# A hybrid encoder layer: four result buffers for SSD, state clears behind their loop, weighted keys on two engines

## Chip, cores and metric

The kernel runs on one core of a Trainium2 chip. The metric is the device time of one execution in microseconds (us). The core's engines each work through a queue of their own, in order: TensorE (PE), VectorE (DVE), ScalarE (ACT), GpSimd (POOL) and SyncE (SP), which here only issues transfers; ScalarE issues some too.

## What is computed

One encoder layer on a sequence of 1024 tokens, 1024 channels, all float32. A normed and modulated input `h` is projected once, four token mixers read parts of the projection, and their outputs, 256 channels each, are normed and joined by one output projection; a SwiGLU feed-forward follows.

```python
h = rms_norm(x) * (1 + sc1) + sh1
u = h @ w_in
y_ssd = ssd_mixer(u[..., :OFF_NA], ...)
y_na = rms_norm(neighborhood_attention(u[..., OFF_NA:OFF_ML], na_rpb), na_norm_g)
y_ml = mlstm_mixer(u[..., OFF_ML:OFF_HY], ...)
y_hy = hyena_mixer(u[..., OFF_HY:], ...)
x = x + g1 * (concatenate([y_ssd, y_na, y_ml, y_hy], -1) @ w_out)
h = rms_norm(x) * (1 + sc2) + sh2
x = x + g2 * ((silu(h @ ffn_w_gate) * (h @ ffn_w_up)) @ ffn_w_down)
return rms_norm(x, final_norm_g)
```

The two mixers that the change touches are SSD and mLSTM. Both work in chunks of 128 tokens, forwards and backwards. In mLSTM a chunk's state is the sum over its tokens of weighted keys times values; the states run through a decay from chunk to chunk; a chunk's result is its queries times the state before it, plus the queries and keys of the chunk itself, weighted by exponentials, times the values. The result is divided by a norm, squared and normed per head, and gated.

## The kernel before

**Stages.** They are written in this order (L349 to L395): modulation and the first norm, Hyena, the projection for SSD (`project_ssd`), the second modulation with its sums, mLSTM's gates and rows, SSD, the projection for mLSTM (`project_ml`), mLSTM (`mlstm`, L1262), the projection for attention (`project_na`), attention and the output projection (`out_round`, L1569, for the mixers' results in the rounds n = 2, 0 and 1), and the feed-forward. The order in which an engine does its work is not the written one: a planner that estimates when each operand is ready interleaves the stages and writes a fixed order for each engine. On the chip an engine never skips an instruction that waits.

**Matrix products.** Float32 operands are split in a high and a low half (`hhi`, `hlo`; `whi`, `wlo`; `yh`, `yl`; `wowh`, `wowl`), and a product is three: high by high, low by high, high by low. L495 (`gemm_t`) and L507 (`gemm_n`) are the projections, with sums in `gps`; L1566 (`out_part`) is the output projection, with sums in `gps` as well. The halves are made by `split` (L233 on ScalarE casts the high one, L239 on VectorE subtracts for the low one).

**SSD's end.** `finish_mixer` (L863) is called by Hyena and by SSD: a root of the mean square (`fss`, `fmv`, `fmt`, `fmr`, L871 and the helper `rsqrt`, L248 to L254), a product on VectorE (L874), then for each of four quarters four transposes on TensorE (`yps`, L879), a copy on ScalarE into the staging tile `yst` (L880), and a store to `yt` in DRAM (L881). SSD's four quarters share one staging buffer (tag `sE`).

**mLSTM.** Three buffers `mkv` take keys and values (L1279); POOL clears the first state of either direction (`mpv`, L1275 and L1276), whose memory was SSD's. For each of 8 chunks POOL weighs the keys in two halves, one for each direction (`mkw`, L1283), and TensorE makes the chunk's states (`mcs`, L1288). After the decay (L1297, VectorE) comes the loop over chunks: `mS` (queries by keys, L1317), `mD` (the exponents, L1322 to L1324), `msd` (the exponential on ScalarE, L1326, and the product on VectorE, L1328), `mpi` (L1335) and `mpa` (L1341) on TensorE, their sum `mtt` on VectorE (L1336, L1342), the norm `mnd` (L1345 to L1347), and on POOL the division (`mhh`, L1349) and the sum of both directions (`my`, L1352). Behind the loop: squares (`msq`, L1356, ScalarE), their sums (`mss`, L1357, VectorE), `rsqrt` on all of it with a table load and a root on ScalarE (`mrv`, `mrt`, `mrr`, L248 to L254, L1359), the product with the gate `mog` (L1366, loaded at L1363) and with the root (L1368), transposes (`yps`, L1374), copies (L1375, three staging buffers) and stores (L1376).

**The output projection's round** loads two slices of weights (`wor`, L1553, scaled at L1554 by `g`), two of a mixer's result (`yr`, L1579) and in the first round the eight tiles of x (L1584); the sums are added to x on VectorE (L1589). The tiles `wor`, `yr`, `yh`, `yl`, `wowh`, `wowl` and x lie in memory that `hhi`, `hlo` and the projection's weights hold until project_na's last matmul. Three buffers in turn take `wor` and `yr`.

Of the kernel before, what the change touches and what calls it, by code (L numbers as in the profile page):

```python
# [9 lines left out]
F32 = mybir.dt.float32  # L10
F32R = mybir.dt.float32r
AF = mybir.ActivationFunctionType
ALU = mybir.AluOpType
# [4 lines left out]
P = 128  # L18
# [267 lines left out]
def build(nc, tc, d, out, dbg=None, dump=None):  # L286
    K = Net(nc, tc, d, out)
    with ExitStack() as es:
# [58 lines left out]
        with ExitStack() as e2:  # L347
# [15 lines left out]
            with ExitStack() as e3:  # L363
                hyena(K, Tags(rpool("hy", e3), n4=2, n2=8, yk=9, tab=3, tai=3, ks=2, rt=2), w0)
# [9 lines left out]
            with ExitStack() as e3:  # L374
                ssd(K, Tags(rpool("ss", e3), cb=6))
            project_ml(K)
            mlstm(K, Tags(rpool("ml", right), va=2))
            project_na(K)
        xr = pool("xr")
# [91 lines left out]
def w_group(K, n, gate=False, first=True):  # L471

    nc = K.nc
    whi, wlo = (K.wp.tile([P, NK, 288 if gate else 256], F32R, t, name=f"{t}{n}") for t in ("whi", "wlo"))
    for j in range(3 if gate else 2):
        w = P if j < 2 else N_GATE
        raw = K.wp.tile([P, NK, w], F32, "raw", name=f"raw{n}")
        nc.sync.dma_start(raw, K.d["w_in"][n + j] if j < 2 else K.d["w_gate"])
        c = slice(j * P, j * P + w)
        with K.first() if first else nullcontext():  # L480
            K.split(whi[:, :, c], wlo[:, :, c], raw, "act", "dve")
    return whi, wlo


def gemm_t(K, whi, wlo, j):

    nc = K.nc
    c = slice(j * P, (j + 1) * P)
    pss = []
    for h in range(2):  # L490
        t = slice(h * 512, (h + 1) * 512)
        ps = K.pg.tile([P, 512], F32, tag="g", name="gps")
        seq = [(w, x, k) for k in range(NK) for w, x in ((whi, K.hhi), (whi, K.hlo), (wlo, K.hhi))]
        for n, (w, x, k) in enumerate(seq):
            nc.tensor.matmul(ps, lhsT=w[:, k, c], rhs=x[k][:, t], start=n == 0, stop=n == len(seq) - 1)  # L495
        pss.append(ps)
    return pss
# [13 lines left out]
def conv3(K, pss, acc, pcol):  # L511

    nc, pc = K.nc, K.pc
    w0, w1, w2, b = (pc[:, pcol + i:pcol + i + 1] for i in range(4))
    m, a = ALU.mult, ALU.add
    with K.first():
        for h in range(2):
            nc.scalar.activation(acc[:, h * 512:(h + 1) * 512], pss[h], AF.Identity, bias=b, scale=w1)
        for o, s, w in ((acc[:, 1:513], pss[0], w0), (acc[:, 513:1024], pss[1][:, :511], w0),
                        (acc[:, 0:511], pss[0][:, 1:512], w2), (acc[:, 511:1023], pss[1], w2)):  # L520
            nc.vector.scalar_tensor_tensor(o, in0=s, scalar=w, in1=o, op0=m, op1=a)
# [299 lines left out]
def hyena(K, sp, w0):  # L821
    nc = K.nc
    V = nc.vector
    z = sp.tile([P, 8, 256], F32, "z")
    late = Late()
    for n in (1, 2, 0):
        whi, wlo = w0 if n == 1 else w_group(K, G_HY + 2 * n)
        for j in range(2):
            pss = gemm_t(K, whi, wlo, j)
            acc = K.so.tile([P, L], F32, "st", name="acc")  # L830
            conv3(K, pss, acc, PC_HYW + 4 * (2 * n + j))
            late.run()
            if n == 0:
                late.add(to_natural, K, acc, z, j)
            else:
                late.add(_natural, K, acc, K.gates[n - 1][j], 0)
    late.run()
    zj = [z[:, :, j * P:(j + 1) * P] for j in range(2)]
    for o in range(2):
        hyena_conv(K, sp, z, o)  # L840
        for j in range(2):
            gate = sp.tile([P, 8, P], F32, "gate")
            nc.sync.dma_start(gate, K.gates[o][j])
            V.tensor_tensor(zj[j], zj[j], gate, op=ALU.mult)
    finish_mixer(K, sp, zj, 2, "n2")


class Late:
# [11 lines left out]
        self.fn = None  # L860


def finish_mixer(K, sp, y, m, tag):  # L863

    nc = K.nc
    ss = sp.tile([P, 2, 8], F32, "fss")
    for i in range(8):
        for j in range(2):
            jk = sp.tile([P, P], F32, "jk", bufs=2)
            nc.scalar.activation(jk, y[j][:, i], AF.Square, accum_out=ss[:, j, i:i + 1])  # L870
    nc.vector.tensor_tensor(ss[:, 0], ss[:, 0], ss[:, 1], op=ALU.add)  # L871
    r = K.rsqrt(sp, ss[:, 0], [P, 8], 256, "fm")
    for j in range(2):
        nc.vector.tensor_tensor(y[j], y[j], r[:, :, None].broadcast_to([P, 8, P]), op=ALU.mult)  # L874
        for h in range(2):
            st = sp.tile([P, 512], F32, tag, name="yst")
            ps = K.pm.tile([P, 512], F32, "m", name="yps")
            for i in range(4):
                nc.tensor.transpose(ps[:, i * P:(i + 1) * P], y[j][:, h * 4 + i], K.ident)  # L879
            nc.scalar.copy(st, ps)  # L880
            nc.scalar.dma_start(K.yt[2 * m + j][:, h * 512:(h + 1) * 512], st)  # L881
# [142 lines left out]
def ssd(K, sp):  # L1024
    nc, d = K.nc, K.d
    V, G = nc.vector, nc.gpsimd
# [54 lines left out]
    pv = sp.tile([P, 8, 2, 2, 2, 64], F32, "spv")  # L1081
# [18 lines left out]
    for i in range(7):  # L1100
        for dr in range(2):
            c, n = (i, i + 1) if dr == 0 else (7 - i, 6 - i)
# [7 lines left out]
    y = pv.rearrange("p c g d h e -> p c (g d h e)")[:, :, 0:256]  # L1110
    for c in range(8):
# [17 lines left out]
        E = sp.tile([P, 512], F32, "sE")  # L1129
# [16 lines left out]
        op = K.pm.tile([P, 512], F32, "m", name="ops")  # L1146
# [12 lines left out]
        for dr in range(2):  # L1159
            G.tensor_tensor(yv, yv, t1v[:, :, dr], op=ALU.add)  # L1160
        V.tensor_tensor(yc, yc, zn, op=ALU.mult)
    finish_mixer(K, sp, [y[:, :, j * P:(j + 1) * P] for j in range(2)], 0, "sE")


def mlstm_rows(K, sp0, sp):
# [96 lines left out]
def mlstm(K, sp):  # L1262
    nc, d = K.nc, K.d
    V, G = nc.vector, nc.gpsimd
    en, wip, emp, dec, gr, M, noneh = K.en, K.wip, K.emp, K.dec, K.gr, K.M, K.noneh
# [6 lines left out]


    pv = sp.tile([P, 2, 8, 2, 65], F32, "mpv")
    G.memset(pv[:, 0, 0], 0.0)  # L1275
    G.memset(pv[:, 1, 7], 0.0)  # L1276
    for c in range(8):
        kv = kvs[c % 3]
        nc.sync.dma_start(kv[:, :, :, 0:64], K.mvk[:, c].rearrange("p n (h e) -> p n h e", h=4))  # L1279
        va, kn = kv[:, 0], kv[:, 1, :, 0:64]  # L1280
        kw = sp.tile([P, 2, 4, 64], F32, "mkw", bufs=2)
        for dr in range(2):
            G.tensor_tensor(kw[:, dr], kn, en[:, c, 2, dr][:, :, None].broadcast_to([P, 4, 64]), op=ALU.mult)  # L1283
        ps = K.pm.tile([P, 512], F32, "m", name="mcs")[:, :260].rearrange("p (d j e) -> p d j e", d=2, j=2)
        for dr in range(2):
            for h in range(4):
                q, j = h % 2, h // 2
                nc.tensor.matmul(ps[64 * q:64 * q + 64, dr, j], lhsT=kw[:, dr, h], rhs=va[:, h], start=True, stop=True)  # L1288
        if c < 7:
            nc.scalar.copy(pv[:, 0, c + 1], ps[:, 0])  # L1290
        if c > 0:
            nc.scalar.copy(pv[:, 1, c - 1], ps[:, 1])
    for i in range(7):
        for dr in range(2):
            c, n = (i, i + 1) if dr == 0 else (7 - i, 6 - i)
            for j in range(2):
                V.scalar_tensor_tensor(pv[:, dr, n, j], in0=pv[:, dr, c, j], scalar=dec[:, dr, c, j:j + 1],  # L1297
                                       in1=pv[:, dr, n, j], op0=ALU.mult, op1=ALU.add)
    y = sp.tile([P, 8, 256], F32, "my")
    for c in range(8):  # L1300
# [30 lines left out]
        for q in range(2):  # L1331
# [6 lines left out]
            for dr in range(2):  # L1338
                for j in range(2):
                    h = 2 * j + q  # L1340
# [28 lines left out]
    for j in range(2):  # L1369
        for h in range(2):  # L1370
            st = sp.tile([P, 512], F32, "msd", bufs=3, name="yst")
# [516 lines left out]
```

## Time and profile before

| | before |
|---|---|
| median of 3 runs | 1519.16 us (1516.4 to 1523.06) |
| the profiled execution | 1516.75 us |
| its span, first to last instruction | 1515.0 us |
| mean granted TensorE clock | 0.973 of full speed |
| TensorE busy | 1388.1 us (92%) |
| VectorE busy | 1114.9 us (74%) |
| ScalarE busy | 542.4 us (36%) |
| GpSimd busy | 90.5 us (6%) |

The span is 1.75 us shorter than the profiled execution's own time. Busy shares are averages over stages with different limits: what a change in one stage is worth is read from that stage's waits and from what stands next on the waiting engine. The stages in question lie between about 590 us (SSD's end) and 710 us (the first rounds of the output projection); mLSTM's first state matmul runs at 608.89 us and its last `mpa` at 674.53 us.

### The profile page before, as it was taken

The page shows a single profiled execution, that of the slowest core. Times are in us where ns is not written, and L with a number is a line of the kernel's source. Part 1 is how long each engine was busy: PE and PEld are TensorE (multiplying, and loading weights), DVE is VectorE, ACT ScalarE, POOL GpSimd, SP SyncE. Part 2 cuts the span into 40 slices and gives each one's busy share as a digit, 9 for nine tenths or more (in the row PEclk, how much of TensorE's full clock was granted, in tenths as well). Part 3 has the DMA queues.
Part 4 walks back from the last instruction along what each step waited for, and adds up shares of the span by engine and source line. Part 5 has one row for each costly group of instructions (what it writes and reads, how often), then busy time and mean ns, then how long its engine had stood idle before and what let it go on. Part 6 is the DMA issues. An engine that isn't in the chain of part 4 may idle for free.

```text
span 1515.0 us, 19511 instructions
## 1 busy us (share of the span) xinstructions
PE 1388.1 (92%) x6717; PEld 1114.2 (74%) x6717; DVE 1114.9 (74%) x2123; ACT 542.4 (36%) x973; POOL 90.5 (6%) x143
## 2 busy tenths in 40 slices
PE   2589989998988999989998999999999999999995
PEld 0366778777777768867776777887778778888884
DVE  7998977887846684587865468478778887557588
ACT  2522222232142343333546766322222222434352
POOL 2110000000100331330000000000000000000000
PEclk9889999999998999999999999999999999999998
DMA  6634367577673332566525458677776676977762
GB/s 249 197 97 150 119 198 222 184 237 232 204 243 100 104 101 91 157 221 209 163 91 189 143 175 278 237 253 247 261 247 223 229 266 240 327 239 243 245 210 111
DMA packets 160598, 300.31 MB, mean 198 GB/s; under 512 B 27871, under 2 KB 72831, under 8 KB 160500
## 3 DMA queue, kind: packets, MB, share of 16 engines
q1 hardware_dynamic: 137204, 271.77, 54.9%
q10 hardware_dynamic: 22688, 25.99, 4.9%
q0 software_dynamic: 608, 1.31, 0.3%
q8 instruction: 53, 0.87, 0.2%
q14 instruction: 45, 0.37, 0.1%
HBM read 221.12 MB, written 77.89 MB: 197 GB/s over the span
## 4 chain that ended last, share of the span: by engine, by line
PE 59%; DVE 14%; DMA 10%; issue 3%; ACT 2%; POOL 2%; SPq 0%; DVEq 0%; POOLq 0%; ACTq 0%
PE Z L1616 8%; PE X L1616 7%; PE dx L1854 6%; PE Y L1616 5%; PE gps L495 4%; PE gps L507 4%; PE dz L1854 4%; PE dy L1854 4%; PE gps L1566 3%; DMA wu<-wu 2%; DMA mxw<-modw 2%; PE nS L1429 2%; PE ops L1566 1%; PE nS L1407 1%; DMA mxacc<-macc 1%
## 5 line engine op out<-in xcount | busy, mean ns | idle before, releaser
L495 PE MATMUL gps<-hhi,whi 128*128 128x512 f32 x320 | 129.8, 406 | 3.8 <-ACT nt L531 3.8
L495 PE MATMUL gps<-hlo,whi 128*128 128x512 f32 x320 | 129.9, 406 | 0.0
L495 PE MATMUL gps<-hhi,wlo 128*128 128x512 f32 x320 | 129.3, 404 | 0.0
L239 DVE TENSOR_TENSOR dl<-dr,dh 128x1024 fp32r<-128x1024 f32 x77 | 93.8, 1221 | 40.7 <-ACT dh L233 32.4
L233 ACT CAST dh<-dr 128x1024 fp32r<-128x1024 f32 x77 | 80.6, 1052 | 108.9 <-PE dx L1854 28.4
L1616 PE MATMUL Z<-hp,wgh 128*128 128x512 f32 x352 | 95.5, 402 | 1.0 <-ACT ps L1671 0.7
L1616 PEld LDWEIGHTS Z<-hp,wgh 128*128 128x128 f32 x352 | 63.7, 188 | 19.0 <-ACT ps L1671 4.4
L507 PE MATMUL gps<-whi,hhi 128*128 128x256 f32 (+1 forms) x256 | 76.1, 297 | 1.5 <-ACT z L531 1.5
L507 PE MATMUL gps<-wlo,hhi 128*128 128x256 f32 (+1 forms) x256 | 77.0, 301 | 0.0
L507 PE MATMUL gps<-whi,hlo 128*128 128x256 f32 (+1 forms) x256 | 76.8, 300 | 0.0
L495 PEld LDWEIGHTS gps<-hhi,whi 128*128 128x128 f32 x320 | 60.6, 189 | 18.6 <-ACT nt L531 5.0
L495 PEld LDWEIGHTS gps<-hhi,wlo 128*128 128x128 f32 x320 | 60.5, 189 | 13.9 <-issue 2.0
L495 PEld LDWEIGHTS gps<-hlo,whi 128*128 128x128 f32 x320 | 60.6, 189 | 13.0 <-issue 1.3
L233 ACT CAST T3h<-wu 128x1024 fp32r<-128x1024 f32 x22 | 23.2, 1052 | 130.8 <-PE Y L1616 120.0
L1616 PE MATMUL X<-A,t4s 128*128 128x512 f32 x264 | 63.5, 389 | 1.3 <-DVE uv L1755 1.3
L1500 DVE SCALAR_TENSOR_TENSOR mxacc<-mxw,cond,mxacc 128x512 f32<-128x512 f32 x56 | 42.0, 750 | 28.2 <-DMA mxw<-modw 28.0
L1616 PEld LDWEIGHTS X<-A,t4s 128*128 128x128 f32 x264 | 49.5, 188 | 11.9 <-DVE uv L1755 1.7
L507 PEld LDWEIGHTS gps<-whi,hhi 128*128 128x128 f32 x256 | 50.4, 197 | 2.7 <-ACT z L531 1.9
L1854 PE MATMUL dx<-dh 128*128 128x512 f32 x132 | 51.3, 389 | 0.0
L1854 PE MATMUL dx<-dh,dl 128*128 128x512 f32 x132 | 51.3, 389 | 0.0
L1854 PE MATMUL dx<-dl,dh 128*128 128x512 f32 x132 | 51.3, 389 | 0.0
L507 PEld LDWEIGHTS gps<-wlo,hhi 128*128 128x128 f32 x256 | 50.2, 196 | 1.6 <-issue 0.7
(521 smaller groups left out, 3499.2 us busy)
## 6 DMA issues: line engine op xcount, KB each, us to landing
wg<-wg SPq DMA_DIRECT2D x44, 512.0 KB
mxw<-modw SPq DMA_DIRECT2D x64, 256.0 KB
raw<-w_in SPq DMA_DIRECT2D x28, 512.0 KB
dr<-wd SPq DMA_DIRECT2D x55, 256.0 KB
psd<-ps SPq DMA_DIRECT2D x22, 512.0 KB
psr<-psd SPq DMA_DIRECT2D x22, 512.0 KB
wu<-wu SPq DMA_DIRECT2D x22, 512.0 KB
ad<-a SPq DMA_DIRECT2D x22, 512.0 KB
```

The costliest lines, as they stand in the source:

```text
L233: nc.scalar.copy(hi, src)
L239: e.tensor_tensor(lo, src, hi.bitcast(F32), op=ALU.subtract)
L495: nc.tensor.matmul(ps, lhsT=w[:, k, c], rhs=x[k][:, t], start=n == 0, stop=n == len(seq) - 1)
L507: nc.tensor.matmul(ps, lhsT=x[k][:, t], rhs=w[:, k, :N], start=n == 0, stop=n == len(seq) - 1)
L1407: nc.tensor.matmul(pb[:, :nk], lhsT=qt[r, i], rhs=ktv[r, r0:r0 + nr, f * 24:f * 24 + 40], start=True, stop=True)
L1429: nc.tensor.matmul(pb[:, 448:512], lhsT=pT[:w * 40, n], rhs=vw[:w * 40, n, c:c + 64], start=n == 0, stop=n == len(chunks) - 1)
L1500: V.scalar_tensor_tensor(acc, in0=mt, scalar=K.cond[:, k:k + 1], in1=acc, op0=ALU.mult, op1=ALU.add)
L1566: K.nc.tensor.matmul(ps, lhsT=l, rhs=r, start=n == 0, stop=n == 5)
L1616: nc.tensor.matmul(ps, lhsT=w[a][:, k], rhs=x[k][b], start=start and n == 0, stop=n == 11, skip_group_check=not start)
L1854: nc.tensor.matmul(acc[i], lhsT=a[:, 0, ts], rhs=b[:, 1], start=first and m == 0, stop=final and m == 2, skip_group_check=n in (2, 3, 5, 6))
```

## The change

SSD's four quarters get four staging buffers, of the tags `sE`, `sW`, `sdm` and `sxd`, whose tiles SSD no longer needs by then; Hyena keeps its one. The two clears of `mpv` are written behind the loop over the states. The weighted keys of the second direction are made on VectorE. From L877 on lines of the changed kernel have a number one higher.

```diff
-    finish_mixer(K, sp, zj, 2, "n2")
+    finish_mixer(K, sp, zj, 2, (("n2", None),))
...
-def finish_mixer(K, sp, y, m, tag):
+def finish_mixer(K, sp, y, m, tags):
...
         for h in range(2):
-            st = sp.tile([P, 512], F32, tag, name="yst")
+            tag, bufs = tags[(2 * j + h) % len(tags)]
+            st = sp.tile([P, 512], F32, tag, name="yst", bufs=bufs)
...
-    finish_mixer(K, sp, [y[:, :, j * P:(j + 1) * P] for j in range(2)], 0, "sE")
+    finish_mixer(K, sp, [y[:, :, j * P:(j + 1) * P] for j in range(2)], 0, (("sE", None), ("sW", None), ("sdm", 2), ("sxd", 2)))
...
     pv = sp.tile([P, 2, 8, 2, 65], F32, "mpv")
-    G.memset(pv[:, 0, 0], 0.0)
-    G.memset(pv[:, 1, 7], 0.0)
     for c in range(8):
...
-        for dr in range(2):
-            G.tensor_tensor(kw[:, dr], kn, en[:, c, 2, dr][:, :, None].broadcast_to([P, 4, 64]), op=ALU.mult)
+        for dr, E in enumerate((G, V)):
+            E.tensor_tensor(kw[:, dr], kn, en[:, c, 2, dr][:, :, None].broadcast_to([P, 4, 64]), op=ALU.mult)
...
         if c > 0:
             nc.scalar.copy(pv[:, 1, c - 1], ps[:, 1])
+    G.memset(pv[:, 0, 0], 0.0)
+    G.memset(pv[:, 1, 7], 0.0)
```

The planner's orders differ from line to line much more than the text does. Three places follow. On TensorE, behind mLSTM's last chunk, there stood before:

```order
L1335 MATMUL mpi<-mpv,mqk 128x130 x2
L1341 MATMUL mpa<-mkv_5072,msd 128x65 x2
L1566 MATMUL gps<-wowh,yh 128x512
L1341 MATMUL mpa<-mkv_5072,msd 128x65 x2
L1335 MATMUL mpi<-mpv,mqk 128x130 x2
L1341 MATMUL mpa<-mkv_5072,msd 128x65 x4
L1566 MATMUL gps<-wowh,yl 128x512
L1566 MATMUL gps<-wowl,yh 128x512
```

and now, from the same point:

```order
L1336 MATMUL mpi<-mpv,mqk 128x130 x2
L1342 MATMUL mpa<-mkv_5072,msd 128x65 x4
L1336 MATMUL mpi<-mpv,mqk 128x130 x2
L1342 MATMUL mpa<-mkv_5072,msd 128x65 x4
L1375 MATMUL yps<-ident,my 128x128 x16
L1567 MATMUL gps<-wowh,yh 128x512 x3
L1567 MATMUL gps<-wowh,yl 128x512
L1567 MATMUL gps<-wowl,yh 128x512
```

Before, 40 matmuls of the output projection stood between the last `mpa` and the first transpose of `my`; now the 16 transposes follow the last `mpa` directly. Ahead of mLSTM, 108 `gps` of L507 stood between the last `gps` of L495 and the first `mcs`; now 60 do, and the other 48 stand among mLSTM's chunks.

On ScalarE, from the last `msd` of mLSTM to the casts of the output projection, before:

```order
L1326 ACTIVATE msd<-mD 128x512 x2
L1356 ACTIVATE msq<-my 128x256
L233 CAST yh<-yr 128x1024
L233 CAST wowh<-wor 128x1024
L1356 ACTIVATE msq<-my 128x256
L249 ACT_TABLE_LOAD
L249 ACTIVATE mrt<-mrv 128x32
L233 CAST wowh<-wor 128x1024
L1375 COPY yst<-yps 128x512
```

and now:

```order
L1327 ACTIVATE msd<-mD 128x512 x2
L1357 ACTIVATE msq<-my 128x256
L976 DMA vn<-no 40x4x256 x2
L1357 ACTIVATE msq<-my 128x256
L249 ACT_TABLE_LOAD
L249 ACTIVATE mrt<-mrv 128x32
L1376 COPY yst<-yps 128x512
L1377 DMA yt<-yst 128x512
L1376 COPY yst<-yps 128x512 x2
L1377 DMA yt<-yst 128x512 x2
L1376 COPY yst<-yps 128x512
L233 CAST wowh<-wor 128x1024
```

The first casts of the output projection (`wowh`, `yh`) moved from ahead of the table load, among mLSTM's last chunks, to behind the four copies of mLSTM's result.

On SP, the loads of mLSTM's last chunks and of the first round of the output projection, before:

```order
L1448 DMA g_6391<-gd 128x1024
L1553 DMA wor<-w_out 128x1024
L1303 DMA mqk<-mqk 128x512
L1306 DMA mkv_5072<-mvk 128x4x64
L1553 DMA wor<-w_out 128x1024
L1579 DMA yr<-yt 128x1024
L1584 DMA x_5_6278<-x 128x1024
L1303 DMA mqk<-mqk 128x512
L1584 DMA x_6_6279<-x 128x1024
L1363 DMA mog<-mon 128x512
```

and now:

```order
L1304 DMA mqk<-mqk 128x512
L1364 DMA mog<-mon 128x512
L1585 DMA x_0_6273<-x 128x1024
L1585 DMA x_1_6274<-x 128x1024
...
L1585 DMA x_6_6279<-x 128x1024
L1449 DMA g_6391<-gd 128x1024
L1554 DMA wor<-w_out 128x1024 x2
L1580 DMA yr<-yt 128x1024
L1585 DMA x_7_6280<-x 128x1024
L1580 DMA yr<-yt 128x1024
```

All loads of x, `g`, `wor` and `yr` now stand behind mLSTM's last load; before, five tiles of x, both `wor` and one `yr` stood ahead of it. The clears of `mpv` stand ahead of the first `mkw` in POOL's order, before and now.

## Rows read from the trace of the kernel before

**Rows 1.** The chain that ended last, whole execution, share by engine.

```profile
PE 59%; DVE 14%; DMA 10%; issue 3%; ACT 2%; POOL 2%; SPq 0%; DVEq 0%; POOLq 0%; ACTq 0%
```

**Rows 2.** Busy time per stretch: stretch, its length, PE, PEld, DVE, ACT, POOL, clock, DMA share, GB/s.

```profile
645.00:650.00 5.00, 4.73 (x31) 3.53 (x30) 4.91 (x14) 2.11 (x4) 1.99 (x3) 1.00 0.95 303
680.00:686.00 6.00, 5.41 (x13) 4.02 (x13) 3.67 (x7) 1.93 (x3) 2.64 (x3) 0.50 0.73 245
710.00:790.00 80.00, 79.95 (x415) 61.23 (x414) 60.74 (x165) 36.44 (x88) 0.00 (x0) 1.00 0.44 134
```

**Rows 3.** PE's waits, 585 to 720 us: line, waited for, total, times, longest.

```profile
PE gps L1566 <- DVE yl L239: 4.1, 3, 2.9
PE mcs L1288 <- POOL mkw L1283: 1.0, 1, 1.0
PE mpa L1341 <- ACT msd L1326: 0.8, 3, 0.3
PE yps L879 <- DVE spv L874: 0.6, 1, 0.6
```

**Rows 4.** The chain in order of time, from 600 us: start, length, what.

```profile
599.96 9.00 PE gps L507 x75
...
695.74 4.50 DMA yr<-yt
...
739.83 6.14 PE gps L1566 x27
```

**Rows 5.** PE's instructions, two chunks of mLSTM: start, length, engine, line, count.

```profile
631.29 0.71 PE L1317 MATMUL mS<-mqk 64*128 64x128 f32 x4
...
638.75 0.72 PE L1317 MATMUL mS<-mqk 64*128 64x128 f32 x8
...
644.75 0.72 PE L1317 MATMUL mS<-mqk 64*128 64x128 f32 x8
```

**Rows 6.** PE's instructions, end of mLSTM and first round; in brackets idle before.

```profile
674.53 1.11 PE L1341 MATMUL mpa<-mkv,msd 128*128 128x65 f32 x8
678.50 0.50 PE L1566 MATMUL gps<-wowh,yl 128*128 128x512 f32 x1 [2.86 <-DVE yl L239]
...
708.43 0.50 PE L1566 MATMUL gps<-wowh,yl 128*128 128x512 f32 x1 [0.64 <-DVE yl L239]
```

**Rows 7.** ACT's instructions.

```profile
594.89 0.59 ACT L880 COPY yst<-yps 128x512 f32<-128x512 f32 x1 [2.12 <-DMA yt<-yst]
...
684.48 0.23 ACT L249 ACTIVATE mrt<-mrv 128x32 f32<-128x32 f32 x1
...
705.29 1.99 ACT L233 CAST yh<-yr 128x1024 fp32r<-128x1024 f32 x2
```

**Rows 8.** POOL's instructions.

```profile
604.88 0.21 POOL L1275 MEMSET mpv<- 128x130 f32 x1 [18.40 <-DMA yt<-yst]
...
609.72 1.21 POOL L1283 TENSOR_TENSOR mkw<-mkv,men 128x256 f32<-128x256 f32 x2 [1.30 <-issue]
...
632.55 1.04 POOL L1349 TENSOR_TENSOR mhh<-mtt,mnd 128x512 f32<-128x512 f32 x1 [9.55 <-DVE mnd L1347]
633.67 0.88 POOL L1352 TENSOR_TENSOR my<-mhh 128x128 f32<-128x128 f32 x2
...
679.85 1.91 POOL L1349 TENSOR_TENSOR mhh<-mtt,mnd 128x512 f32<-128x512 f32 x1 [4.19 <-DVE mnd L1347]
681.84 0.87 POOL L1352 TENSOR_TENSOR my<-mhh 128x128 f32<-128x128 f32 x2
```

**Rows 9.** DVE's instructions.

```profile
589.11 0.20 DVE L250 RECIPROCAL fmr<-fmt 128x8 f32<-128x8 f32 x1 [1.15 <-ACT fmt L249]
...
631.40 0.43 DVE L1342 TENSOR_TENSOR mtt<-mtt,mpa 128x260 f32<-128x260 f32 x1
...
679.69 1.17 DVE L239 TENSOR_TENSOR yl<-yr,yh 128x1024 fp32r<-128x1024 f32 x1
...
690.61 2.78 DVE L1368 TENSOR_TENSOR my<-my,mrr 128x256 f32<-128x256 f32 x8
```

## Prediction

> **What bounds the kernel now.** I began with the chain that ended last: TensorE carries most of it [rows 1], so the question for every part of the change is whether PE's idle time grows or shrinks. Then one stretch without idle time behind the changed stages: from 710 to 790 us PE is busy 79.95 of 80 us at full clock [rows 2]. A microsecond that PE is late at 710 is therefore still missing at the end; no slack takes it up. Third, PE's waits between 585 and 720 us [rows 3]: only 0.6 us stand in SSD's finish (L879), where the first part of the change works; 1.0 stands at the state matmuls `mcs`, where the third part works, and 0.8 at `mpa`. The large one, 4.1 us in three pieces, stands behind mLSTM: the out-projection's first round waits for `yl`. The whole stock that the change aims at is thus below 3 us; what it could lose lies at the end of mLSTM. Fourth, the instructions themselves around 609 us [rows 4], in two chunks of mLSTM [rows 5], and at its end [rows 6].
>
> **SSD's four result buffers.** Before, ScalarE's second copy waits 2.12 us for the first store [rows 7], and the copies end late; POOL's `mpv` clears sit idle until 604.88 us for these stores [rows 8]. With four buffers those waits go. By themselves they are worth nothing: ScalarE has slack, and PE streams `gps` (project_na) all the while. What they do is let the planner start mLSTM sooner: on PE 60 `gps` of L507 stand behind the last one of L495 and ahead of the first `mcs`, where 108 stood. 48 fewer at 9.00 / 75 = 0.12 us [rows 4] is 5.76 us. Those 48 are not saved; they move into mLSTM's stage as filler, 72 in 25 pieces between the last `mcs` and the last `mpa`, where there were 24 in 5 pieces and four out-projection matmuls in 3.
>
> **The clears.** Written behind the loop, they still stand ahead of the weighted keys in POOL's order, so this part is costed at nothing; what covers it is that the clears take 0.21 us and the stores they wait for land sooner. If that cover goes, see the third rival.
>
> **The weighted keys.** A pair takes 1.21 us on POOL [rows 8]; with one half on DVE it takes the longer half, about 0.6 us, so `mcs` gets its keys 0.6 sooner. The DVE half of the same shape should be near the 0.4 us of DVE's other operations of this stage (`mtt`, [rows 9]); eight of them are 3.4 us of an engine that has gaps there. PE's 1.0 us wait can shrink by 0.6; ends 0 and 1.0. Beside this the trace shows the two engines in each other's way: POOL's `mhh` takes 1.91 us at 679.85, while DVE runs `yl` and `mnd`, against 1.04 at 632.55 [rows 8]. The Trainium skill (SBUF — State Buffer, "SBUF: two separate sides") speaks against the split: a DVE operation with two SBUF inputs and a GpSimd operation that reads SBUF exclude each other for a whole instruction. The trace agrees: `yl` ran from 679.69 for 1.17 us [rows 9], and 1.0 of it after `mhh`'s start is about what `mhh` took longer. By that rule the halves run one after the other, 0.4 + 0.6 us, the gain falls from 0.6 to 0.2 us, and the sum rises by 0.4.
>
> **Inside mLSTM.** The filler closes waits: 0.6 at `mcs` and 0.8 at `mpa`, together -1.4 (ends 0 and -1.8). Every piece of filler between the small matmuls also costs a break: the chunk from 631.29 to 638.75 us holds 8 `gps` in 4 pieces and takes 7.46 us, the next takes 6.00 [rows 5], of which 0.3 is a wait at `mpa` [rows 3]. 7.46 - 8 x 0.12 - 5.7 = 0.8, or 0.2 a piece; had the filler closed no wait, 0.12. I take 0.16. Twenty-five pieces against eight are +2.7 (ends 0 and 3.4). Net **+1.3**. So mLSTM's last `mpa` ends about when it did, 675.6 us [rows 6]: I call this T.
>
> **The end of mLSTM.** This is the term that decides. Before, the out-projection's loads and casts ran during mLSTM's last chunks, since project_na's last matmuls stood in mLSTM's second chunk and so freed the memory early; behind T, PE had 40 `gps` to do while DVE, POOL and ScalarE finished mLSTM's norm, and idled 4.1 us less the 0.64 at 708 us, 3.45 [rows 3, 6]. Now project_na's last matmul stands in the last but one chunk, all x, `wor` and `yr` loads stand on SP behind mLSTM's last load, and PE's order behind the last `mpa` is: all 16 transposes of mLSTM's result, then the first out-projection matmul. PE must sit through the whole chain, counted from T. From the start of `mtt` to the end of the second `my` it was 631.40 [rows 9] to 634.55 [rows 8] before: **3.2**. Square, sum, table load and root went from the end of `my` at 682.71 [rows 8] to 684.71 [rows 7]: **5.2**. Six small DVE operations at 0.2 each (as the reciprocal at 589.11 [rows 9]) make it **6.5**, eight products, 2.78 [rows 9], **9.3**. PE's transposes run half behind the first four products and half after the last, to **10.8**. ScalarE copies four results out; the fourth waits for a buffer (three exist) until the first store has landed, some 2.1 us after its copy (by the wait of 2.12 in [rows 7]), and ends at **11.7**. Only then come its casts `wowh`, `wowh`, `yh` at 1.0 each (`yh` x2, 1.99 [rows 7]), to **14.8**, where PE does three matmuls. DVE's `wowl`, `wowl`, `yl`, 1.2 each (`yl`, 1.17 [rows 9]), start when the first cast is done at 12.7 and end at **16.4**; PE gets three more. The second `yr` takes a buffer that the first `wowl` frees at 14, and a `yr` load took 4.50 [rows 4]: **18.5**; its cast and `yl` make **20.8**, and from there PE runs on.
>
> In those 20.8 us PE does 11 matmuls at 6.14 / 27 [rows 4] and 16 transposes, taken at the 0.12 of the 256-column `gps`, 4.4 us in all; idle is 16.4. Against 3.45 before: **+12.9**. Ends: +9 (the second `yr` and `yl` hidden) and +17 (loads late, below).
>
> **Clock.** After the gaps of before the granted clock is 0.50 from 680 to 686 us [rows 2], the 1.2 GHz level, with PE idle for 2.86 us ahead of it: some 3 us lost. The gap is longer now and the same slow stretch follows: **+0.3** (ends 0 and +3, if it is paid twice, round the transposes and again at 20.8).
>
> **Border of the first two rounds.** The second round's casts stand on ScalarE behind attention's squares, a table load and a root, where before PE waited 0.64 us [rows 6]. Ends 0 and +2; I take **+1.0**, near the middle, since the order moved but the 3 us of casts are the same.
>
> **Sum:** +1.3 + 12.9 + 0.3 + 1.0 = **+15.5 us**. The profiled execution took 1516.75, which gives 1532.3; the median of the runs shown is 2.4 us higher and would give 1534.7. I forecast **1533**, between the two.
>
> **Rivals.**
> 1. Filler is free (not slower). Were mLSTM's chunks paced by ScalarE's exponentials and DVE rather than PE, the 48 matmuls would cost nothing there: -5.8 and -2.7 to the sum, +7.0 us, about **1525**, within what a measurement can tell. It decides if a chunk with nine or ten `gps` stays near 6.1 us. For it: DVE is busy 4.91 of 5 us at 645 us [rows 2]. Against: the chunk with eight `gps` took 7.46, and a chunk shows 0.3 us of PE wait at most [rows 3]. Chance 0.12.
> 2. The loads are late too. Seven x tiles, g, two `wor` and `yr` are 5.5 MB; at 303 GB/s [rows 2] some 18 us, and they can start only when project_na has ended and mLSTM's last load is issued. I put that 9 us ahead of T, so that all is there when wanted. Were it at T - 4, `wor` comes 4 to 5 us late: **1538**. Chance 0.14.
> 3. mLSTM is not ready sooner. If the clears still wait until 604.88, the first keys come at 605.8, but PE stands at the first `mcs` at 603.1: +3 us, **1536**. Against: with four buffers the fourth store should land near 599. Chance 0.07.
> 4. Something that shortens the tail, as a start of the out-projection ahead of the transposes; PE's order speaks against it. Faster than 1516: 0.05.
>
> **Numbers.** Forecast 0.62, the rivals as above. The range runs from 1524 (rival 1, and the low ends of tail and border) to 1541 (late loads with the half clock paid twice). A measurement tells some 0.5%, 7.6 us, from no change. Slower: the forecast and rivals 2 and 3, 0.83. Same: rival 1, 0.12. Faster: 0.05.
>
> **What would show it.** Right: the first `mcs` at about 603 and without a long wait; chunks of mLSTM near 7.3 us; the last `mpa` within 2 us of 675.6; behind it 9 to 10 us of PE idle until the transposes, then waits for `yh` and `yl`, 16 us in all; granted clock 0.50 near 690 to 700. Wrong: a chunk with filler at 6.1 us, an idle time behind T below 9 us, or PE waits after 710 that shrink by as much as the tail grows.

## The result and the profile after

| | before | changed |
|---|---|---|
| median | 1519.16 us (7 runs, 1516.4 to 1523.06) | 1531.17 us (7 runs, from 1525.5) |
| the profiled execution | 1516.75 us | 1528.52 us |
| its span | 1515.0 us | 1526.7 us |
| mean granted clock | 0.973 | 0.973 |
| TensorE busy | 1388.1 us | 1387.6 us |

The changed kernel takes 1.0071 times as long, with an interval from 1.0047 to 1.0095. One of its seven runs took 4135 us; the ratios leave it out, as they do every run more than 1.5% above the fastest of its kernel, and without it the median is 1529.85 us. A second series beside other runs (e10 below) gave 1.0095 (1.0071 to 1.0119). TensorE does the same work; it waits more.

To find where, follow three points in TensorE's order that both kernels share: the first transpose of SSD's result, mLSTM's last `mpa`, and the first `ops` of attention's output projection; ahead of the first point and from the third to the end TensorE's order is the same. The two views by tile say when the instructions of a tile begin first and last. Before:

```profile
L1341 PE MATMUL mpa<-mkv,msd x128: 217/275/324, 628.0 to 675.4; 128*128 128x65 f32 x128
```
```profile
L1566 PE MATMUL ops<-now,ny x96: 388/389/477, 783.9 to 890.5; 128*128 128x512 f32 x96
```

and in the changed kernel:

```profile
L1342 PE MATMUL mpa<-mkv,msd x128: 217/275/324, 620.8 to 672.0; 128*128 128x65 f32 x128
```
```profile
L1567 PE MATMUL ops<-now,ny x96: 388/389/478, 795.1 to 902.1; 128*128 128x512 f32 x96
```

From the last `mpa` to the first `ops` it was 783.9 - 675.4 = 108.5 us and is now 795.1 - 672.0 = 123.1: 14.6 us more. From SSD's first transpose (591.5 before, 589.9 now) to the last `mpa` it was 83.9 and is 82.1 us, 1.8 less. Together 12.8 us are lost between SSD's end and the first `ops`. What lies outside takes 1.1 us of that back; executions differ there by several us, with the same orders (SSD's first transpose begins at 589.8 us in e8 and at 596.0 in e6).

TensorE's waits from 585 to 720 us, now, to compare with [rows 3]:

```profile
PE yps L1375 <- DVE my L1369: 7.3, 1, 7.3
PE gps L1567 <- ACT yh L233: 5.5, 2, 5.2
PE yps L880 <- DVE spv L874: 0.6, 1, 0.6
PE mcs L1287 <- POOL mkw L1282: 0.5, 1, 0.5
```

The waits at `mpa` are gone and the one at `mcs` halved; in place of 3.45 us behind the last `mpa` [rows 6] stand 7.3 us at mLSTM's transposes and 5.5 at the first matmuls of the output projection. The instructions there:

```profile
671.14 1.10 PE L1342 MATMUL mpa<-mkv,msd 128*128 128x65 f32 x8
679.51 3.88 PE L1375 MATMUL yps<-ident,my 128*128 128x128 f32 x16 [7.26 <-DVE my L1369]
688.58 1.65 PE L1567 MATMUL gps<-wowh,yh 128*128 128x512 f32 x3 [5.19 <-ACT yh L233]
...
692.13 0.80 PE L1567 MATMUL gps<-wowh,yh 128*128 128x512 f32 x1 [0.26 <-ACT yh L233]
```

And the stretches of 5 us from 671 on, with the columns of [rows 2]; the third column from the end holds the granted clock:

```profile
671.00:676.00 5.00, 1.25 (x10) 0.98 (x9) 2.02 (x8) 0.53 (x2) 1.90 (x3) 0.67 0.89 272
676.00:681.00 5.00, 1.49 (x5) 0.91 (x6) 4.10 (x16) 1.40 (x3) 0.00 (x0) 0.50 1.03 416
681.00:686.00 5.00, 2.39 (x12) 1.91 (x12) 3.10 (x5) 2.55 (x5) 0.00 (x0) 0.80 0.77 297
686.00:691.00 5.00, 2.42 (x5) 1.52 (x6) 3.50 (x3) 2.53 (x3) 0.00 (x0) 0.54 0.55 199
691.00:696.00 5.00, 4.74 (x13) 2.79 (x11) 1.70 (x2) 2.33 (x2) 0.00 (x0) 0.50 0.86 340
696.00:701.00 5.00, 5.00 (x22) 3.69 (x23) 2.35 (x5) 0.00 (x0) 0.00 (x0) 0.94 1.05 307
```

TensorE is busy 1.25 to 2.42 of 5 us for 20 us. The clock is at 0.50, the 1.2 GHz level, in two pieces: from 672.7 to 683.0 us, and again from 686.4 to 696.6, when the matmuls have come back. Before there was one such piece, from 679.3 to 686.1.

### The profile page after: what moved, and what is told of

Same layout as the page of the kernel before. It is cut to its first block, busy times and chain, and to the rows that moved or that the text cites. A ratio compares the mean times of both kernels' runs of the same rounds, so it can differ in the third digit from the quotient of the medians.

```text
span 1526.7 us, 19520 instructions
## 1 busy us (share of the span) xinstructions
PE 1387.6 (91%) x6717; PEld 1112.6 (73%) x6717; DVE 1117.2 (73%) x2131; ACT 542.1 (36%) x973; POOL 83.1 (5%) x135
## 3 DMA queue, kind: packets, MB, share of 16 engines
q0 software_dynamic: 608, 1.31, 0.3%
## 4 chain that ended last, share of the span: by engine, by line
PE 66%; DVE 17%; DMA 10%; issue 3%; ACT 2%; POOL 1%; SPq 0%; DVEq 0%; POOLq 0%; ACTq 0%
PE Z L1617 8%; PE gps L495 8%; PE dx L1855 6%; PE X L1617 6%; PE Y L1617 5%; PE gps L507 5%; PE gps L1567 4%; PE dz L1855 4%; PE dy L1855 4%; DMA wu<-wu 2%; DMA mxw<-modw 2%; PE nS L1430 2%; PE ops L1567 1%; PE nS L1408 1%; DMA sx<-wd 1%
## 5 line engine op out<-in xcount | busy, mean ns | idle before, releaser
L495 PE MATMUL gps<-hhi,whi 128*128 128x512 f32 x320 | 128.8, 403 | 3.8 <-ACT nt L531 3.8
L495 PE MATMUL gps<-hlo,whi 128*128 128x512 f32 x320 | 129.4, 404 | 0.0
L495 PE MATMUL gps<-hhi,wlo 128*128 128x512 f32 x320 | 129.0, 403 | 0.0
L1617 PEld LDWEIGHTS Z<-hp,wgh 128*128 128x128 f32 x352 | 63.7, 188 | 19.8 <-ACT ps L1672 4.3
L507 PE MATMUL gps<-whi,hhi 128*128 128x256 f32 (+1 forms) x256 | 76.0, 297 | 1.5 <-ACT z L531 1.5
L507 PE MATMUL gps<-whi,hlo 128*128 128x256 f32 (+1 forms) x256 | 76.7, 300 | 0.0
L507 PE MATMUL gps<-wlo,hhi 128*128 128x256 f32 (+1 forms) x256 | 76.5, 299 | 0.0
L495 PEld LDWEIGHTS gps<-hhi,whi 128*128 128x128 f32 x320 | 60.2, 188 | 18.5 <-ACT nt L531 5.0
L495 PEld LDWEIGHTS gps<-hhi,wlo 128*128 128x128 f32 x320 | 60.2, 188 | 13.7 <-issue 2.0
L495 PEld LDWEIGHTS gps<-hlo,whi 128*128 128x128 f32 x320 | 60.2, 188 | 12.8 <-issue 1.3
L507 PEld LDWEIGHTS gps<-whi,hhi 128*128 128x128 f32 x256 | 49.5, 193 | 3.3 <-ACT z L531 1.9
L1617 PE MATMUL Y<-AS,T3h 128*128 128x512 f32 x176 | 45.5, 401 | 6.8 <-DVE uv L1752 6.8
```

The source lines that it names most:

```text
L507: nc.tensor.matmul(ps, lhsT=x[k][:, t], rhs=w[:, k, :N], start=n == 0, stop=n == len(seq) - 1)
L1617: nc.tensor.matmul(ps, lhsT=w[a][:, k], rhs=x[k][b], start=start and n == 0, stop=n == 11, skip_group_check=not start)
```

## The experiments

Theory A says that the loss is TensorE's idle time behind mLSTM, and that the four buffers alone cause it, by the order that the planner then writes. Theory B says that the keys on two engines cost it. The table gives each run's ratio to before, and for its profiled execution the two stretches of above (PE, from the first transpose of SSD's result to the last `mpa`, and from there to the first `ops`). In e4 and e5 all of project_na's value matmuls stand ahead of the first point, so their first stretch compares only with each other's.

| run | ratio (interval) | SSD's end to last `mpa` | last `mpa` to first `ops` |
|---|---|---|---|
| before | 1 | 83.9 us | 108.5 us |
| the change | 1.0071 (1.0047 to 1.0095) | 82.1 | 123.1 |
| e1 four buffers only | 1.0050 (1.0019 to 1.0081) | 82.2 | 123.5 |
| e2 clears and keys only | 1.0005 (0.9978 to 1.0033) | 88.9 | 108.5 |
| e3 change, project_na ahead | 1.0020 (0.9989 to 1.0051) | 88.9 | 108.5 |
| e4 before, project_na first | 1.0238 (1.0204 to 1.0271) | 98.4 | 109.3 |
| e5 change, project_na first | 1.0159 (1.0117 to 1.0202) | 92.9 | 108.7 |
| e6 change, fourth result buffer | one run, 1532.58 us | 83.2 | 123.3 |
| e7 before, loads first | 1.0047 (1.0019 to 1.0075) | 93.0 | 108.5 |
| e8 change, both | 1.0056 (1.0025 to 1.0086) | 100.2 | 105.6 |
| e9 before again | one run, 1516.09 us | 84.4 | 108.5 |
| e10 the change again | 1.0095 (1.0071 to 1.0119) | 81.8 | 123.6 |
| e11 change, two buffers more | 1.0068 (1.0042 to 1.0094) | 83.2 | 120.3 |
| e12 e3 again | 1.0031 (0.9995 to 1.0066) | 91.6 | 108.6 |

### e1 and e2: the parts apart

e1 is the change without its other two parts:

```diff
-        for dr, E in enumerate((G, V)):
-            E.tensor_tensor(kw[:, dr], kn, ...)
+        for dr in range(2):
+            G.tensor_tensor(kw[:, dr], kn, ...)
```

with the clears ahead of the loop again; e2 is these two parts alone, on the kernel before.

> Only SSD's four result buffers; clears and weighted keys as before. PE's and ScalarE's orders are those of the changed kernel. Theory A (the loss is PE's idle time behind mLSTM's last mpa, and the buffers alone cause it, through the order): 12 us slower than before, some 1531, ratio 1.007 to 1.009; PE waits about 7.3 us at mLSTM's transposes and 5 us for yh; the wait at mcs is 0.5 to 1.5 us. Theory B (the keys on two engines cost it, DVE and POOL in each other's way): the time of before within 3 us, 1519.

> Only the moved clears and the weighted keys on two engines; SSD's result through one buffer. PE's order is that of before. Theory A: 0 to 1 us faster than before, 1518 to 1519, since only the 1.0 us wait at mcs can go; 40 output-projection matmuls cover mLSTM's end and PE idles about 3.5 us there. Theory B: slower by most of the change's 12 us, 1529 or so, with long mkw operations on POOL.

TensorE's waits in e1, from 585 to 720 us:

```profile
PE yps L1375 <- DVE my L1369: 7.3, 1, 7.3
PE gps L1567 <- ACT yh L233: 6.0, 2, 5.7
...
PE mcs L1289 <- POOL mkw L1284: 0.3, 1, 0.3
```

The change's waits stand in e1 to 0.5 us, and its last stretch is 123.5 us; in e2 that stretch is 108.5, as before, and the time is that of before. So the buffers alone bring the longer stretch, and theory B falls. In time e1 is slower than before, clear of noise, but its 1.0050 lies below the 1.007 to 1.009 that I gave; only its interval reaches them. The view of the weighted keys' tile in the changed kernel shows what the split does (shortest, median and longest, ns):

```profile
L1282 POOL TENSOR_TENSOR mkw<-mkv,men x8: 612/626/862, 596.2 to 612.9; 128x256 f32<-128x256 f32 x8
L1282 DVE TENSOR_TENSOR mkw<-mkv,men x8: 409/423/828, 599.5 to 612.9; 128x256 f32<-128x256 f32 x8
```

Some of these operations get in each other's way. At 610.25 us both halves of one pair start, and POOL's takes 0.86 us instead of 0.61:

```profile
610.25 0.43 DVE L1282 TENSOR_TENSOR mkw<-mkv,men 128x256 f32<-128x256 f32 x1
```
```profile
610.29 0.86 POOL L1282 TENSOR_TENSOR mkw<-mkv,men 128x256 f32<-128x256 f32 x1 [2.13 <-DVE mpv L1298]
```

At 602.41 it is the other way round: POOL's half had begun 0.08 us before, and DVE's takes 0.83 us instead of 0.42:

```profile
602.41 0.83 DVE L1282 TENSOR_TENSOR mkw<-mkv,men 128x256 f32<-128x256 f32 x1
```

That is the direction that the Trainium skill (SBUF — State Buffer, "SBUF: two separate sides") states; the 0.25 us added to POOL's half are less than the 0.4 for which the rule would have it wait. PE's wait at `mcs` is 0.5 us with the split and 0.3 without it: the third part is worth nothing here.

### e3 and e12: the change, with more of project_na ahead of mLSTM

project_na's eight value tiles are cut in two, and the first four written ahead of mLSTM:

```diff
+            na = project_na(K, 4)
+            next(na)
             mlstm(K, Tags(rpool("ml", right), va=2))
-            project_na(K)
+            for _ in na:
+                pass
...
+            if h * 4 + i == cut:
+                yield
             ps = gemm_n(K, whi, wlo, h * 4 + i, 256)
```

> All three parts of the change, and the first four of the eight 128-row tiles of project_na's value part written ahead of mLSTM: 96 gps ahead of the first mcs, 65 among the states, 31 among the chunks, and 40 output-projection matmuls behind the last mpa again. Theory A: the loss goes, time of before within 3 us (1516 to 1521); PE idle behind the last mpa 3 to 4 us as before. Theory B, or a loss that the early start of mLSTM brings by itself: still 8 us or more over before, 1527 or more.

> e3 again, unchanged, since its interval and the change's nearly touch. If four value tiles ahead of mLSTM give back most of the loss: 0.998 to 1.004 of before, the stretch from the last mpa to the first ops 108 to 109 us as in e3 (123 in the change), and what is over in the stretch ahead of it goes with the clock in mLSTM's chunks. If they do not: 1.006 or more.

The last stretch is back at 108.5 and 108.6 us, with all three parts of the change in place, and the waits behind the last `mpa` are those of before:

```profile
PE gps L1579 <- DVE yl L239: 2.9, 1, 2.9
PE mcs L1299 <- POOL mkw L1294: 1.7, 3, 0.9
PE mpa L1354 <- ACT msd L1339: 0.8, 2, 0.5
```

So what the last stretch loses goes with the order of project_na against mLSTM, and with the loads and casts that follow from that order; the keys and the clears do not bring it. In time, each interval still overlaps the change's; the two series together, 1.0025 against 1.0083 for the change and e10, lie apart, with half widths of 0.0024 and 0.0017 if the series are taken as independent. Both runs end 0.2 to 0.3% over before, with intervals that hold 1: whether something remains is not settled. In their profiled executions it lies ahead of the last `mpa`, with the clock (see the end).

### e4 and e5: what the buffers are worth where something waits for them

Here project_na's value part gets raised priority, on the kernel before (e4) and on the change (e5):

```diff
-    _nat_cols(K, G_NA + 4, lambda o, i: nc.scalar.copy(o, i), store)
+    with K.first():
+        _nat_cols(K, G_NA + 4, lambda o, i: nc.scalar.copy(o, i), store)
```

> The kernel before (no part of the change), with project_na's value part at raised priority: no gps of it is left for mLSTM's stage, 17 output-projection matmuls stand among the chunks and 58 behind the last mpa. Theory A (what counts is how much work PE has ready behind the last mpa): PE idle behind it 0 to 2 us instead of 3.45, up to 3 us of half clock less; against that the states' loop has no filler and PE waits 3 to 8 us there for keys and loads. Between 4 us faster and 6 us slower than before. If filler among the states were worth nothing, 5 us faster.

> As e4, project_na's value part at raised priority, but with all three parts of the change. In e4 PE waited 19.8 us for the first yh, with ScalarE's copies of SSD's result held up by the stores of one buffer (5.4, 4.3 and 3.8 us) and its casts queued behind them. If the four buffers are worth what they take away where something waits behind them: this wait falls to 10 to 15 us (then the loads of wor and yr decide) and the time is 4 to 10 us below e4, some 1550, ratio 1.016 to 1.022. If the buffers are worth nothing by themselves in any order: as e4, 1557.

My expectation of e4 missed by 30 us. The planner put three matmuls of the output projection ahead of the first `mcs`; their `yh` is cast on ScalarE behind the four copies of SSD's result, and each copy waits for the store before it. ScalarE's and PE's instructions in e4:

```profile
626.49 0.58 ACT L880 COPY yst<-yps 128x512 f32<-128x512 f32 x1 [5.42 <-DMA yt<-yst]
...
631.35 0.58 ACT L880 COPY yst<-yps 128x512 f32<-128x512 f32 x1 [4.28 <-DMA yt<-yst]
...
635.74 0.58 ACT L880 COPY yst<-yps 128x512 f32<-128x512 f32 x1 [3.80 <-DMA yt<-yst]
```
```profile
640.23 1.65 PE L1567 MATMUL gps<-wowh,yh 128*128 128x512 f32 x3 [19.80 <-ACT yh L233]
```

With four buffers the copies follow each other (618.32 to 620.43 us), and the planner no longer puts those three matmuls ahead of the first `mcs`:

```profile
618.32 1.07 ACT L881 COPY yst<-yps 128x512 f32<-128x512 f32 x2
...
619.85 0.58 ACT L881 COPY yst<-yps 128x512 f32<-128x512 f32 x1 [0.47 <-ACT yst L881]
```
```profile
PE mcs L1288 <- POOL mkw L1283: 18.1, 4, 14.2
```

PE now waits at `mcs` for keys, 14.2 us once where it had been 19.8, since nothing is left to fill that place. The ratio falls from 1.0238 to 1.0159, some 12 us, more than the 4 to 10 that I gave it, but the two intervals only just stay apart. Of the 14.6 us between the two profiled executions 6.1 stand in the two stretches; the rest lies outside them. Neither order is a good one; but with the change, and the order that the planner writes for it, the stretches are some 6 us shorter where PE's next instruction hung on the copies. In e3, whose order is near that of before, nothing is gained by the buffers. No run changes the buffers with PE's order held as it is.

### e6 and e11: the chain behind the last mpa

```diff
-            st = sp.tile([P, 512], F32, "msd", bufs=3, name="yst")
+            st = sp.tile([P, 512], F32, *(("msd", "yst", 3) if j * h == 0 else ("mkw", "yst", 2)))
```

is e6; e11 has besides

```diff
-        raw = S.tile([P, L], F32, W_RAW, "yr")
+        raw = S.tile([P, L], F32, 17 if first and j else W_RAW, "yr")
```

> The changed kernel, with a fourth staging buffer for mLSTM's result (a tile of the mkw tag). Theory A (the casts of the output projection queue on ScalarE behind the fourth copy, which waited 1.6 us for a store): that wait is gone, the casts come 1.6 us sooner, PE's wait for the first yh falls from 5.2 to about 3.6 us, and the stretch from the last mpa to the first ops is 1 to 2 us shorter. If the loads of wor and yr decide instead, the wait stays near 5.

> The changed kernel, with a fourth staging buffer for mLSTM's result and a fourth buffer for the first round's loads, so that its second yr need not wait for the first wowl. PE's order at mLSTM's end stays that of the change. Theory A (the chain behind the last mpa as in the prediction): the second yh comes right behind the first, PE runs on 3 to 4 us sooner, the stretch from the last mpa to the first ops is 3 to 5 us shorter than the change's 122.9, and the ratio to before 1.003 to 1.006. If the loads of x ahead of wor and yr decide: no shorter than the change.

e6 missed, because it did not take the delay away. The fourth copy no longer waits for a store's end, but it stands 1.33 us behind the issue of the second and third store. The third's issue took 1.21 us, where it took 0.34 in the change:

```profile
690.28 1.70 ACTq L1377 DMA_DIRECT2D yt<-yst  x2
692.08 0.58 ACT L1376 COPY yst<-yps 128x512 f32<-128x512 f32 x1 [1.33 <-issue]
```

The copy ends 13.2 us behind the last `mpa`, 13.5 in the change, and the last stretch of this one run is 123.3 us; what the wait is worth stays open. In e11 the second `yh` follows the first at once, where the change waits 2.50 us for its load:

```profile
690.90 1.99 ACT L233 CAST yh<-yr 128x1024 fp32r<-128x1024 f32 x2
```
```profile
691.03 1.04 ACT L233 CAST yh<-yr 128x1024 fp32r<-128x1024 f32 x1 [2.50 <-DMA yr<-yt]
```

and the stretch falls by 3.3 us, to 120.3 from the 123.6 of e10, in the range that was expected (by 2.8 from the 123.1 of the change's first profile, just below it). So the chain behind the last `mpa` sets the length of the stretch, and a link of it taken out comes back there. The times do not settle it: the ratio is 1.0068 against e10's 1.0095, with intervals that overlap, and it is a little over what I gave.

### e7 and e8: filling the end of mLSTM

Both raise the priority of the first round's weights and results; e8 is on the change, with six value tiles ahead of mLSTM as in e3.

```diff
+    with K.first() if first else nullcontext():
     w = load_wo(K, S, ct, ...)
     ys = []
     for j in range(2):
```

(what follows in the loop over `j` included).

> The kernel before (no part of the change), with the weights and results of the output projection's first round (wor, yr, their casts and subtractions) at raised priority: 20 of its matmuls stand among mLSTM's chunks (4 before) and 66 behind the last mpa (40 before). Theory A (PE's ready work behind mLSTM decides): the idle behind the last mpa falls from 3.45 to 0 to 1 us, the half clock behind it goes, 3 to 7 us faster than before, ratio 0.995 to 0.998. If the idle there is a matter of mLSTM's own chain: no change.

> All three parts of the change, six of project_na's eight value tiles ahead of mLSTM, and the output projection's first loads and casts at raised priority: 144 gps ahead of the first mcs, 48 among the states, none among the chunks, 30 output-projection matmuls among the chunks and 63 behind the last mpa. Theory A: no idle behind the last mpa beyond 1 us, no half clock there, 3 to 8 us faster than before (1512 to 1517), 15 us faster than the changed kernel. If the early start of mLSTM or the keys on two engines cost by themselves: not below 1519.

Both missed. In e7 the place behind the last `mpa` is filled, as expected, by one run of 66 matmuls without a wait (the chain in order of time):

```profile
684.46 15.07 PE gps L1566 x66
```

but then other waits stand in the same 108.5 us:

```profile
PE yps L1461 <- DVE nq L1460: 4.3, 1, 4.3
PE gps L1566 <- ACT yh L233: 2.3, 1, 2.3
PE nS L1407 <- DMA nk<-kt: 1.3, 1, 1.3
PE mpa L1341 <- issue: 1.1, 1, 1.1
```

The second round's `yh` (2.3) and attention's operands (1.3 and 4.3) are now late: the matmuls that went ahead are missing there. And the 16 more among mLSTM's chunks, with the half clock that follows the wait of 1.1 us up to 659.86, make the stretch ahead of the last `mpa` 9.1 us longer. In e8 no filler stands in mLSTM's first four chunks, and the clock is 0.67 from 640 to 660 us; that the one brings the other is not shown, since before has four chunks without filler too, at 1.00. Where PE's ready work is short, to move it is to move the gap. No version here beats the kernel before; e2 equals it.

### e9 and e10: both kernels again

> The kernel before, unchanged, profiled a second time. In e2, whose TensorE order is that of before, the granted clock fell to 0.50 in mLSTM's chunks (650 to 660 us) without a wait of PE over 0.3 us ahead of it; in the first profile of before it stayed at 1.00 there. If that fall comes and goes between executions of one program: the stretch from SSD's transposes to the first ops differs from the first profile's 192.4 us by up to 6 us, with the clock below 1.00 somewhere between 620 and 670 us, or it is again 192 to 193 us with the clock at 1.00. If the fall in e2 belongs to its keys on two engines: 192 to 193 us and 1.00 throughout.

> The changed kernel, unchanged, beside before and e11 on one chip. 1.005 to 1.009 of before. In its profile 12 to 14 us of PE idle behind the last mpa and the clock at 1.00 through mLSTM's chunks, if a dense filler keeps it there; below 1.00 somewhere between 620 and 670 us, if the filler does nothing for the clock.

e9 has 192.9 us over both stretches, as in the first profile, yet the clock did fall among its chunks:

```profile
660.00:665.00 5.00, 4.97 (x34) 4.20 (x34) 4.94 (x16) 2.44 (x4) 1.91 (x3) 0.84 0.96 333
665.00:670.00 5.00, 4.63 (x21) 3.36 (x20) 3.52 (x9) 2.45 (x4) 1.91 (x3) 0.81 0.74 260
```

e10's ratio, 1.0095, is just over the 1.005 to 1.009 that I gave. Its clock stayed at 1.00 through mLSTM, with 14.4 us of waits behind the last `mpa`, border included. That looked like the work of the dense filler; e11, with the same filler, has 0.67 at 650 to 655 us, PE busy 5.00 of 5. So the filler does not hold the clock by itself.

## Why the prediction was right

The forecast was 1533 in a range from 1524 to 1541, the measured median 1531.17; the sum said +15.5 us against the profiled execution, which came out at +11.8, and +12.8 over the stretches that it covers.

**The start.** 48 `gps` fewer ahead of the first `mcs` were to bring it 5.76 us forward; from SSD's first transpose it was 17.4 us and is 11.6. The clears begin at 593.43 us, so the third rival is out.

```profile
593.43 0.21 POOL L1292 MEMSET mpv<- 128x130 f32 x1 [8.60 <-DMA yt<-yst]
```

**Inside mLSTM** I took +1.3; it was -0.8. This is the term that was mis-sized: 2.1 of the 2.7 us by which the sum is over the 12.8. From the first `mcs` to the end of the last `mpa` it takes 70.75 us instead of 66.75; 48 matmuls more at 0.12 and four less at 0.23 are +4.8. Waits of 1.6 us closed (2.1 with the 0.3 at `mpi` before, 0.5 now), about as taken. A break costs less than 0.16: the last chunk, without filler, takes 5.78 us (666.46 to 672.24), all eight take 56.78 (from 615.46), and 56.78 - 8 x 5.78 - 72 x 0.12 = 1.9 us for 25 pieces, 0.08 each. The chunk of [rows 5] had misled me: by the trace it holds 7 `gps` in 3 pieces, not 8 in 4, and one piece stands among its `mS`. In the changed kernel the four chunks of that kind take 0.6 us more than 5.78 and their `gps`, the three others with filler 0.2 less.

```profile
615.46 0.72 PE L1318 MATMUL mS<-mqk 64*128 64x128 f32 x8
```
```profile
666.46 0.72 PE L1318 MATMUL mS<-mqk 64*128 64x128 f32 x8
```

The first rival, free filler, is out as well: the chunks with filler take 6.4 to 8.6 us in the change, and those with 9 and 11 `gps` 7.5 and 7.7, not 6.1.

**The end of mLSTM** went link by link as in the prediction, counted from the last `mpa`'s end at 672.24: root 5.2 (5.2 predicted), products 9.5 (9.3), transposes 11.2 (10.8), fourth copy 13.5 (11.7), first `yh` 16.3 (14.8), second `yr` 18.8 (18.5), second `yl` 21.1 (20.8). The copy is late because the store that it waits for took 3.4 us, not 2.1 (681.61 to 685.03), and the transposes ran at half clock. Two of these links:

```profile
685.11 0.59 ACT L1376 COPY yst<-yps 128x512 f32<-128x512 f32 x1 [1.61 <-DMA yt<-yst]
```
```profile
692.11 1.23 DVE L239 TENSOR_TENSOR yl<-yr,yh 128x1024 fp32r<-128x1024 f32 x1 [1.94 <-ACT yh L233]
```

The loads were there in time: `wor` is scaled directly behind the products, so the second rival is out. (Its eleven tiles of 512 KB are 5.8 MB, not 5.5, and at 303 GB/s 19 us, not 18.)

**Idle and clock** share the loss otherwise than I had it: the waits behind the last `mpa` grew by 12.7 - 3.45 = 9.3 us, not 12.9, and the half clock took some 3.2 us more, not 0.3 (what is left of 14.6 after these 9.3, the 1.2 below, and 0.9 for the four matmuls that now stand behind the last `mpa`). PE's 16 transposes took 3.88 us, twice the 1.9 that I took, inside the same 20 us. "+3, if it is paid twice" stood there as an end; it was paid twice. The sum of both is 12.5 against 13.2. For the most part these are not two misses that happened to cancel. Up to 19.9 us behind the last `mpa`, where PE's last wait in the chain ends (692.13), the chain sets the time; PE's 16 transposes and 6 matmuls took 7.2 us of it, where I had 4.4 us for 16 and 11, and what they took more came off the idle time.

**The border** was +1.0; waits of 1.2 and 0.8 us stand there now, against 0.84 before: +1.2.

```profile
PE gps L1567 <- ACT yh L233: 1.2, 1, 1.2
PE gps L1567 <- DVE yl L239: 0.8, 1, 0.8
```

**The signs.** Most came out, three did not. The last `mpa` ended at 672.24, not within 2 us of 675.6; counted from SSD's first transpose it is 1.8 us early, and e10 has it at 675.63. PE was idle 7.3 us up to the transposes, not 9 to 10: the prediction's own chain has the first four products done 7.9 us behind the last `mpa`, so this sign did not follow from it. Read as that one wait, the sign "below 9 us" spoke for being wrong; all the waits there make 12.7, less than the 16 I gave.

## What to carry to other kernels

Where a planner orders each engine's work by readiness, taking a wait away upstream can let a stage start sooner, and what was going to fill that stage's end is then spent earlier in it: compare the orders, and look at what the bounding engine has ready at the end of the stage, before counting the wait as gain. The same waits were worth nothing in one order here and some 6 us of two stretches in another, so price a wait in the order that is written. Work that is moved into a gap is missing where it came from.

## What the runs showed of the hardware that was not expected

The granted clock falls among mLSTM's chunks in some executions of a program and not in others. In e2, whose PE order is that of before, it was 1.00 up to 645 us, then:

```profile
645.00:650.00 5.00, 5.00 (x30) 4.36 (x31) 3.54 (x11) 0.42 (x1) 0.09 (x1) 0.73 0.95 310
650.00:655.00 5.00, 5.00 (x18) 3.72 (x16) 3.28 (x9) 2.01 (x4) 1.98 (x3) 0.50 0.66 252
655.00:660.00 5.00, 5.00 (x23) 4.33 (x23) 2.69 (x8) 0.00 (x0) 0.00 (x0) 0.50 0.34 89
```

with no wait over 0.3 us in the 5 us ahead of it, and its stretch up to the last `mpa` took 5.0 us more than in the first profile of before. e3, e6, e9, e11 and e12 have such falls at other places of the same chunks. What sets them off is open. The `mS` matmuls of the chunk ahead of the fall and of the chunk behind it, eight of one shape, show either level:

```profile
641.63 0.72 PE L1317 MATMUL mS<-mqk 64*128 64x128 f32 x8
...
647.90 1.23 PE L1317 MATMUL mS<-mqk 64*128 64x128 f32 x8
```

A store's issue can hold ScalarE's queue: the third store of mLSTM's result took 1.21 us to issue in e6 and 1.31 in e10, where it took 0.34 in the change, and in e6 the copy behind it waited for no semaphore that the profile shows. What held it is open.
